# A two-layer float32 decoder trunk: factors 1 and 5 of the seven-product down projection in the mixers' score tiles, block sums in tiles of their own, rotary tables five chunks later

## The chip, the core and the metric

The kernel runs on one core of one Trainium2 chip. A core has a matrix engine (TensorE, PE in the profile), a vector engine (DVE), a scalar engine (ACT) and a general engine (POOL), with one instruction queue each and an on-chip memory that they share; SP is a fifth queue that here only issues loads. Each queue runs its instructions in the order in which they stand in it, and an instruction waits, with all that is behind it in its queue, for the semaphores of the work that it depends on. Matrix products land in PSUM banks, from which DVE and ACT read.

The metric is the device time of one launch in microseconds (us). The kernel before took 2172.97 us as the median of three runs (2170.84 to 2173.14).

## The reference, cut to what matters

Two layers; x is 512 tokens of width 1024, everything in float32. Weights of a layer are 1024 by 2816 for the gated feed-forward blocks.

```python
def swiglu(x, w_gate, w_up, w_down):
    return (jax.nn.silu(x @ w_gate) * (x @ w_up)) @ w_down

for l in range(DEPTH):                                   # DEPTH = 2
    h = h + 0.5 * swiglu(rmsnorm(h, ffn1_norm[l]), ffn1_w_gate[l], ffn1_w_up[l], ffn1_w_down[l])
    z = rmsnorm(h, mix_norm[l]) @ w_in[l]                # columns go to four mixers
    y_a = mla_mixer(...)                                 # latent attention, rotary phases
    y_b = spatial_gating_mixer(...)
    y_c = hgrn2_mixer(...)                               # gated linear recurrence
    y_d = retention_mixer(...)                           # rotary phases, decay
    h = h + jnp.concatenate([y_a, y_b, y_c, y_d], axis=-1) @ w_out[l]
    h = h + 0.5 * swiglu(rmsnorm(h, ffn2_norm[l]), ffn2_w_gate[l], ffn2_w_up[l], ffn2_w_down[l])
    gate = jax.nn.sigmoid(rmsnorm(h, ple_norm[l]) @ ple_w_gate[l])
    h = h + (p[l] @ ple_w_proj[l]) * gate
return rmsnorm(h, final_norm)
```

## The kernel before, in words

**Layout and precision.** The residual stream h lies on chip as eight tiles of 128 features by 512 tokens. Every dense product is made of three float32r products: each operand is split into a rounded high part (a cast, on ACT) and a low rest (a subtraction, on DVE); `parts` (L126) does this, and `mm3` (L171) issues high x high, high x low and low x high (L173, L174, L175).

**Feed-forward block.** `ffn` (L290) walks 22 chunks of 128 hidden features, in parts of 8, 8 and 6 (`PARTS`). `hidden` (L298) makes one chunk: two weight loads of 512 KB by `weights` (L131, SP queue), split into wh and wl, 24 matmuls each for gate and up into the PSUM tiles `gu`, and four evacuation steps (L309 to L312). There are four PSUM banks for them, so the gate product of a chunk can start only when L309 of the chunk two before has read its bank. Parts of 8 chunks go to `down7` (L316), the part of 6 to a plain down projection. There are four feed-forward blocks, so `down7` runs eight times.

**The down projection in seven products.** `down7` multiplies the hidden features with the down weights in 2 by 2 blocks with seven block products instead of eight. The right factors are made of the hidden chunks: hb1 carries those of products 1 and 5, hb2 of 2 and 3, hb3 of 6 and 7, hb4 of 4 (L318 to L337). hb1 is done with the first four chunks; hb2, hb3 and hb4 need the last four. The left factors are weight blocks and sums of them; `seven` (L142) makes them for one pair of output tiles, i and i + 4, and there are four pairs. It loads the two halves of the first block row into a `raw` tile (r1, r2), two of the blocks of the second row into s1 and s3, adds a second block to each of s1 and s3 with an accumulating load on POOL's queue (L157, L158), and loads a last block into a22. `keep` (L146) then splits each factor into a tile `ws` of 128 by 1024, high and low side by side; between these, DVE adds s1 to r1 (L162) and r1 to r2 (L165). Factor 1 is r1, 5 is s1, 2 is r2, 6 is r1 + s1, 3 is r2 + r1 + s1, 7 is s3, 4 is a22. A product is 12 matmuls (L353) into dx, dy or dz, and DVE adds each result to h (L359).

The 28 products stand in an order written by hand (L361): (1,0), (5,0), (1,1), (5,1), (2,0), (6,0), (3,0), (7,0), (2,1), (4,0) and so on, product and pair.

**Tiles.** A pool tag has a fixed number of buffers, and a tile waits until a buffer of its tag is free. Tag `w` has 6 buffers (weights wh and wl, and factors 1, 5, 2, 4); `raw` has 3; `st` has 4 (the mixers' score tiles, and factors 6, 3, 7); `t` has 7 tiles of 128 by 512 (g, gq, squares, and s1, s3, a22); `r` has 3 (row scales, and the token positions while the tables are made); `vx` has 1 and `sc` has 2 (mixers).

**The order of work.** A scheduler orders each queue when the program is built, by priority and by when it expects buffers and results; weights and their splits are marked urgent (L98). So the place of an instruction follows from the buffers too.

**Rotary tables.** `tables` (L389) makes three sine tables and four products of them, on DVE, ACT and one memset on POOL. It runs once, called in the first feed-forward block when chunk 4 has been made (L313), and the mixers use it.

Of the kernel before, what the change touches and what calls it, by code (L numbers as in the profile page):

```python
# [10 lines left out]
F32 = mybir.dt.float32  # L11
F32R = mybir.dt.float32r
# [7 lines left out]
P = 128  # L20
D = 1024
T = 512
# [8 lines left out]
HS = 4  # L31
# [19 lines left out]
WB = 1024  # L51
# [9 lines left out]
def trunk(ctx, tc, xT, pT, pos, wgu, wdn, winT, winN, wout, wpg, wpp, wmla,  # L61
# [8 lines left out]
    tp = ctx.enter_context(tc.tile_pool(name="temps", bufs=1))  # L70
# [5 lines left out]
    def nm(s):  # L76
        uid[0] += 1
        return f"{s}{uid[0]}"
# [2 lines left out]
        return up.tile(list(shape), dt, tag="u", bufs=24, name=nm(name))  # L81

    def t2(shape=(P, T), dt=F32, name="t"):
        return tp.tile(list(shape), dt, tag="t", bufs=7, name=nm(name))

    def stile(name="st"):
        return tp.tile([P, 10, P], F32, tag="st", bufs=4, name=nm(name))
# [32 lines left out]
    def wtile(name):  # L120
        return wp.tile([P, WB], F32R, tag="w", bufs=6, name=nm(name))

    def rtile():
        return wp.tile([P, WB], F32, tag="raw", bufs=3, name=nm("wr"))

# [16 lines left out]
    def seven(a1, a2):  # L142

        w = {}

        def keep(n, p, src):  # L146
            t = wtile("ws") if n % 7 < 4 else tp.tile([P, 10 * P], F32R, tag="st", bufs=4, name=nm("ws"))
            w[p] = t[:, 0:WB].rearrange("p (e c) -> p e c", e=2)
            parts(w[p][:, 0], w[p][:, 1], src)

        with urgent():
            s1, s3, raw, a22 = t2(name="s1"), t2(name="s3"), rtile(), t2(name="a22")
            r1, r2 = raw[:, 0:T], raw[:, T:WB]
            nc.sync.dma_start(out=s1, in_=a2[:, 0:T])
            nc.sync.dma_start(out=s3, in_=a1[:, 0:T])
            nc.sync.dma_start(out=raw, in_=a1)
            nc.gpsimd.dma_start(out=s1, in_=a2[:, T:WB], accum_op=ALU.add)  # L157
            nc.gpsimd.dma_start(out=s3, in_=a2[:, 0:T], accum_op=ALU.add)  # L158
            nc.sync.dma_start(out=a22, in_=a2[:, T:WB])
            keep(0, 1, r1)  # L160
            keep(1, 5, s1)
            dve.tensor_tensor(r1, r1, s1, op=ALU.add)  # L162
            keep(2, 2, r2)
            keep(4, 6, r1)
            dve.tensor_tensor(r2, r2, r1, op=ALU.add)  # L165
            keep(5, 3, r2)
            keep(6, 7, s3)
            keep(3, 4, a22)
        return w

    def mm3(o, a, b, start, stop, go_on=False):  # L171
# [51 lines left out]
    def row_rsqrt(acc, n, last=None, v=None):  # L223

        a = [t2(dt=F32R, name="ac") for _ in range(2)]
        act.copy(a[0], acc)
        dve.tensor_tensor(a[1], acc, a[0].bitcast(F32), op=ALU.subtract)
        q = mps("ms")
        for i in range(2):
            pe.matmul(q, lhsT=onesr, rhs=a[i], start=i == 0, stop=i == 1)  # L230
        return ln_rsqrt(q, n, tp.tile([P, T], F32, tag="r", bufs=3, name=nm("r")), last,
                        v is not None and (v, t2(name="rt")))

    def ln_rsqrt(q, n, r, last=None, vt=None):

        v, t = vt or (t2(name="rv"), t2(name="rt"))
        dve.tensor_scalar(v, q, 1.0 / n, EPS, op0=ALU.mult, op1=ALU.add)
        i = act.preload_act_table_set("natural_log_exp_and_others")
        if last is not None:
            after(i, last)  # L240
        after(act.activation(t, v, AF.Ln), i)
        after(act.activation(r, t, AF.Exp, scale=-0.5), i)
        newton_step(v, r, t)
        return r
# [10 lines left out]
    class Norm:  # L255
# [20 lines left out]
        def scale(self, cols=False):  # L276
            with urgent():
                if not cols:
                    self.r = row_rsqrt(self.acc, D, self.last)
                    return self.r  # L280
                self.vx = tp.tile([P, T], F32, tag="vx", bufs=1, name=nm("vx"))
                self.r = row_rsqrt(self.acc, D, self.last, v=self.vx)
                c = columns(self.r, "rc")
                c2 = sp.tile([P, NB], F32, tag="rc2", bufs=1, name=nm("rc2"))
                dve.tensor_tensor(c2, c, c, op=ALU.mult)
                self.rc = [c, c2]
            return self.r


    def ffn(idx, norm, done, first=None, nextw=None, hook=None):  # L290
        x = norm.x
        r = norm.scale()
        rh = tp.tile([P, T], F32, tag="r", bufs=3, name=nm("rh"))
        act.mul(rh, r, 0.5)
        H = T // 2
        lo_, hi_ = slice(0, H), slice(H, T)
# [1 line left out]
        def hidden(f, g):  # L298
            ps = []
            for m in range(2):  # L300
                if first:
                    ps.append(first.pop(0))
                    continue
                w = nextw.pop(0) if nextw else weights(wgu[idx, f, m])
                o = dense("gu")
                for k in range(KD):
                    mm3(o, wpart(w, k * P), xpart(x[k]), k == 0, k == KD - 1)
                ps.append(o)
            dve.tensor_tensor(g, ps[0], r, op=ALU.mult)  # L309
            act.activation(g, g, AF.Silu)  # L310
            dve.tensor_tensor(g, g, ps[1], op=ALU.mult)  # L311
            dve.tensor_tensor(g, g, rh, op=ALU.mult)  # L312
            if f == 4 and hook is not None:  # L313
                hook()

        def down7(f0):  # L316
# [50 lines left out]
        for n in PARTS:  # L367
# [9 lines left out]
            for m in range(KD):  # L377
                w = weights(wdn[idx, m, :, f0 * P:(f0 + n) * P], n * P)
# [9 lines left out]

    def tables():  # L389
        pin = t2((P, T), I32, name="pin")  # L390
        posf = tp.tile([P, T], F32, tag="r", bufs=3, name="posf")
        nc.scalar.dma_start(out=pin, in_=pos)
        dve.tensor_copy(posf, pin)

# [76 lines left out]
    def mixers(l, norm, done):  # L471
        x = norm.x
        r = norm.scale(True)
# [96 lines left out]
        class Hgrn:  # L570
# [3 lines left out]
            def __init__(self, b, q, kk, ff, wait):  # L574
                self.b, self.q, self.k = b, q, kk
                self.st = stile("hst")[:, 0:8].rearrange("p (e j) t -> p e (j t)", e=2)
                pool.memset(self.st, 0.0)
                self.sc = tp.tile([P, 8, 32], F32, tag="sc", bufs=2, name=nm("sc"))
                dve.tensor_tensor(self.sc, self.near(wait),
                                  cs[:, K_D32:K_D32 + 32].unsqueeze(1).to_broadcast([P, 8, 32]), op=ALU.mult)  # L580
                dve.tensor_tensor(q, q, ff, op=ALU.mult)
                self.d = ff.rearrange("p e t -> p (e t)")
                self.d2 = stile("hd").rearrange("p a t -> p (a t)")
                self.at = 0
# [258 lines left out]
        for b in range(2):  # L843
            pts = []
            for e in range(2):
# [3 lines left out]
                for i in range(NB):  # L849
                    n = (i + 1) * P  # L850
# [42 lines left out]
        for b in range(2):  # L893
            st = [ret_scores(rq_[64 * e:64 * e + 64, b], rk_[64 * e:64 * e + 64, b]) for e in range(2)]
# [2 lines left out]
        yd = group_norm(od, norm.vx, C_RET + 2 * l)  # L897


        rw = t2((P, 256), name="rows")  # L900
        nc.scalar.dma_start(out=rw, in_=rows[l])
        ws = t2((P, HS, P), name="ws")
        after(nc.scalar.dma_start(out=ws, in_=sgw[l]), mla_end)
        bs = sp.tile([P, HS], F32, tag="bs", bufs=1, name=nm("bs"))
        nc.scalar.dma_start(out=bs, in_=sgb[l])
# [41 lines left out]
        for m in range(KD):  # L947
            w = weights(wout[l, m])
# [99 lines left out]
    for _ in range(20):  # L1048
        pe.matmul(o[:, 0:2 * P], lhsT=wide[:, 0:P], rhs=wide, start=True, stop=True)
    raw = [rtile() for _ in range(2)]  # L1050
    hi, lo = ([wtile(f"w{c}0") for _ in range(2)] for c in "hl")
    first = [dense("gu") for _ in range(2)]
    prev = None
    for k in range(KD):
        prev = inturn(nc.sync.dma_start(out=h[k], in_=xT[:, k, :]), prev)
        norm.x[k] = split(h[k], gain(V_FFN1, k))
        for m in range(2):
            if k % 2 == 0:
                c = slice(k * P, (k + 2) * P)
# [4 lines left out]
    with urgent():  # L1064
        for m in range(2):
            w, hi, lo = unit(shape=(P, WB), name="wr"), wtile("wh1"), wtile("wl1")
            for k in range(0, KD, 4):
                c = slice(k * P, (k + 4) * P)
# [133 lines left out]
```

## Time and profile before

| what | value |
|---|---|
| runs | 2172.97 us median, 2170.84 to 2173.14 (3 runs) |
| the profiled execution | 2168.55 us |
| its span on the core | 2166.8 us, 30799 instructions |
| busy, PE / DVE / ACT / POOL | 2105.4 / 1386.0 / 885.5 / 77.3 us |
| mean granted TensorE clock | 0.988 |
| moved by DMA | 224.65 MB |

The page of the profile gives, for one execution on the chip, busy times by engine, the chain of work that ended last, and groups of instructions. "PE gu L173" is a matmul into tile gu at line 173; "dy<-hb,ws" is a product that reads hb and ws. In a list of waits, "PE dy L173 <- ACT ws L127: 26.6, 8, 3.3" says that PE stood still before a matmul of line 173 into dy until ACT had finished a cast into ws, 26.6 us in all, 8 times, 3.3 us at most. In a timeline a row is start, duration, engine, line, operation, and in brackets the idle time before it and what ended it. In a row of windows, PEclk is the granted clock (1.00 is full speed), and "DMA share" the busy share of the core's 16 DMA engines.

### The profile page before, as it was taken

The numbers are of one execution on the slowest core, as the hardware profiler recorded it, in microseconds if no ns is written. First come the engines' busy times: TensorE is split into PE (matmuls) and PEld (weight loads), VectorE is DVE, ScalarE is ACT, GpSimd is POOL, SyncE is SP. The second block draws the span as 40 slices with busy tenths as digits, with TensorE's granted clock in tenths as the row PEclk, the third lists the DMA queues.
The fourth block names the chain that finished last, engine by engine and source line by source line (L and its number), as shares of the span: only waits on it lengthen the run. The fifth ranks groups of instructions, "written<-read, shape, count | busy, mean of one in ns | idle before, by whom it ended". The sixth has DMA issues, their size and how long they took to land.

```text
span 2166.8 us, 30799 instructions
## 1 busy us (share of the span) xinstructions
PE 2105.4 (97%) x12392; PEld 1767.9 (82%) x12392; DVE 1386.0 (64%) x2286; ACT 885.5 (41%) x1379; POOL 77.3 (4%) x109
## 2 busy tenths in 40 slices
PE   8999999999999999999999999999999999999997
PEld 6788888877788798888887988888777888888887
DVE  6775755776675575745766657467766657557476
ACT  5333423625544333423544333245445534233252
POOL 0000100001000000100000001000010001000000
PEclk9999999999999999999999999999999999999999
DMA  4352622322122442523235335232221226235231
GB/s 159 112 139 93 150 98 88 104 73 82 58 78 98 112 132 98 147 96 98 98 107 139 105 111 142 84 102 93 70 90 45 89 97 154 95 117 132 88 124 52
DMA packets 79375, 224.65 MB, mean 104 GB/s; under 512 B 9472, under 2 KB 13056, under 8 KB 79232
## 3 DMA queue, kind: packets, MB, share of 16 engines
q1 hardware_dynamic: 66320, 200.98, 28.2%
q0 software_dynamic: 10240, 18.88, 5.4%
q10 hardware_dynamic: 2672, 2.82, 0.4%
q8 instruction: 97, 1.59, 0.3%
q14 instruction: 46, 0.38, 0.1%
HBM read 218.45 MB, written 2.10 MB: 102 GB/s over the span
## 4 chain that ended last, share of the span: by engine, by line
PE 92%; DVE 4%; ACT 2%; issue 1%; DMA 0%; SPq 0%; DVEq 0%; ACTq 0%
PE gu L173 15%; PE gu L174 15%; PE gu L175 15%; PE z L173 3%; PE z L174 3%; PE z L175 3%; PE dx L173 3%; PE dx L174 3%; PE dx L175 3%; PE dn L173 2%; PE dn L174 2%; PE dn L175 2%; PE dy L175 2%; PE dy L173 1%; PE dy L174 1%; PE y L173 1%
## 5 line engine op out<-in xcount | busy, mean ns | idle before, releaser
L127 ACT CAST wh<-wr 128x1024 fp32r<-128x1024 f32 (+3 forms) x307 | 307.8, 1004 | 730.8 <-issue 318.2
L173 PE MATMUL gu<-x,wh 128*128 128x512 f32 x1408 | 549.3, 391 | 9.4 <-DVE g L309 6.9
L174 PE MATMUL gu<-x,wh 128*128 128x512 f32 x1408 | 549.7, 391 | 0.2
L175 PE MATMUL gu<-x,wl 128*128 128x512 f32 x1408 | 549.5, 390 | 0.0
L128 DVE TENSOR_TENSOR wl<-wr,wh 128x1024 fp32r<-128x1024 f32 (+3 forms) x307 | 356.5, 1163 | 56.8 <-ACT wh L127 52.0
L173 PEld LDWEIGHTS gu<-x,wh 128*128 128x128 f32 x1408 | 265.3, 188 | 65.5 <-issue 4.0
L174 PEld LDWEIGHTS gu<-x,wh 128*128 128x128 f32 x1408 | 265.4, 189 | 56.5 <-DVE x L203 1.7
L175 PEld LDWEIGHTS gu<-x,wl 128*128 128x128 f32 x1408 | 265.1, 188 | 55.5
L311 DVE TENSOR_TENSOR g<-g,gu 128x512 f32<-128x512 f32 x88 | 60.4, 687 | 285.4 <-PE gu L175 279.6
L173 PE MATMUL dx<-hb,ws 128*128 128x256 f32 x512 | 147.1, 288 | 1.2 <-DVE h L359 1.2
L174 PE MATMUL dx<-hb,ws 128*128 128x256 f32 x512 | 146.2, 286 | 0.0
L175 PE MATMUL dx<-hb,ws 128*128 128x256 f32 x512 | 144.6, 285 | 0.0
L309 DVE TENSOR_TENSOR g<-gu,r 128x512 f32<-128x512 f32 x88 | 60.6, 689 | 113.4 <-PE gu L175 113.3
L173 PE MATMUL z<-x,wh 128*128 128x512 f32 x320 | 127.8, 399 | 0.0
L174 PE MATMUL z<-x,wh 128*128 128x512 f32 x320 | 126.6, 396 | 0.0
L175 PE MATMUL z<-x,wl 128*128 128x512 f32 x320 | 126.2, 394 | 0.0
L127 ACT CAST hb<-g 128x256 fp32r<-128x256 f32 (+1 forms) x128 | 58.7, 459 | 138.7 <-DVE g L312 90.1
L127 ACT CAST ws<-wr 128x512 fp32r<-128x512 f32 x128 | 78.8, 619 | 73.6 <-PE gu L174 27.8
L173 PE MATMUL dy<-hb,ws 128*128 128x256 f32 x256 | 77.6, 303 | 26.6 <-ACT ws L127 26.6
L173 PEld LDWEIGHTS dx<-hb,ws 128*128 128x128 f32 x512 | 100.2, 196 | 2.1 <-DVE h L359 1.7
L174 PEld LDWEIGHTS dx<-hb,ws 128*128 128x128 f32 x512 | 100.1, 195 | 0.3
L175 PEld LDWEIGHTS dx<-hb,ws 128*128 128x128 f32 x512 | 99.0, 194 | 0.0
(358 smaller groups left out, 3677.8 us busy)
## 6 DMA issues: line engine op xcount, KB each, us to landing
wr<-in_wgu SPq DMA_DIRECT2D x172, 512.0 KB, 3.2
wr<-in_winT SPq DMA_DIRECT2D x40, 512.0 KB, 3.2
wr<-in_wdn SPq DMA_DIRECT2D x32, 512.0 KB, 3.6
s<-in_wdn SPq DMA_DIRECT2D x64, 256.0 KB, 4.2
s<-in_wdn POOLq DMA_DIRECT2D x64, 256.0 KB, 5.2
wr<-in_wdn SPq DMA_DIRECT2D x32, 384.0 KB, 3.1
a<-in_wdn SPq DMA_DIRECT2D x32, 256.0 KB, 3.7
wr<-in_winN SPq DMA_DIRECT2D x16, 512.0 KB, 3.3
```

The lines of the kernel that those rows point to most:

```text
L127: i = act.copy(hi, src)
L128: dve.tensor_tensor(lo, src, hi.bitcast(F32), op=ALU.subtract)
L173: i = pe.matmul(o, lhsT=a[0], rhs=b[0], start=start, stop=False, skip_group_check=go_on)
L174: pe.matmul(o, lhsT=a[0], rhs=b[1], start=False, stop=False, skip_group_check=go_on)
L175: pe.matmul(o, lhsT=a[1], rhs=b[0], start=False, stop=stop, skip_group_check=go_on)
L309: dve.tensor_tensor(g, ps[0], r, op=ALU.mult)
L311: dve.tensor_tensor(g, g, ps[1], op=ALU.mult)
```

## The change

It moves tiles between buffers and one call in time; no arithmetic is added or left out.

- Factors 1 and 5 of a pair go into `st` buffers, the other five into `w` buffers (before: 6, 3, 7 in `st`; 1, 5, 2, 4 in `w`). The weights of the first chunk go into `st` buffers too.
- s1 and s3 get a tag of their own, `side`, with 4 buffers; the mixers' vx, sc, rows and spatial weights and the token positions use it as well. In return `t` has 6 buffers, `r` has 2, and `vx` and `sc` are gone.
- The tables are called at chunk 9 instead of chunk 4 of the first block.

```diff
     def t2(shape=(P, T), dt=F32, name="t"):
-        return tp.tile(list(shape), dt, tag="t", bufs=7, name=nm(name))
+        return tp.tile(list(shape), dt, tag="t", bufs=6, name=nm(name))
...
+    def spare(name):
+
+        return tp.tile([P, 10 * P], F32R, tag="st", bufs=4, name=nm(name))
+
+    def side(shape=(P, T), name="sd"):
+        return tp.tile(list(shape), F32, tag="side", bufs=4, name=nm(name))
...
-        def keep(n, p, src):
-            t = wtile("ws") if n % 7 < 4 else tp.tile([P, 10 * P], F32R, tag="st", bufs=4, name=nm("ws"))
-            w[p] = t[:, 0:WB].rearrange("p (e c) -> p e c", e=2)
+        def keep(p, src, n=1):
+            w[p] = (wtile("ws") if n else spare("ws"))[:, 0:WB].rearrange("p (e c) -> p e c", e=2)
             parts(w[p][:, 0], w[p][:, 1], src)
 
         with urgent():
-            s1, s3, raw, a22 = t2(name="s1"), t2(name="s3"), rtile(), t2(name="a22")
+            s1, s3, raw, a22 = side(name="s1"), side(name="s3"), rtile(), t2(name="a22")
...
-            keep(0, 1, r1)
-            keep(1, 5, s1)
+            keep(1, r1, 0)
+            keep(5, s1, 0)
             dve.tensor_tensor(r1, r1, s1, op=ALU.add)
-            keep(2, 2, r2)
-            keep(4, 6, r1)
+            keep(2, r2)
+            keep(6, r1)
             dve.tensor_tensor(r2, r2, r1, op=ALU.add)
-            keep(5, 3, r2)
-            keep(6, 7, s3)
-            keep(3, 4, a22)
+            keep(3, r2)
+            keep(7, s3)
+            keep(4, a22)
...
-        return ln_rsqrt(q, n, tp.tile([P, T], F32, tag="r", bufs=3, name=nm("r")), last,
+        return ln_rsqrt(q, n, tp.tile([P, T], F32, tag="r", bufs=2, name=nm("r")), last,
...
-                self.vx = tp.tile([P, T], F32, tag="vx", bufs=1, name=nm("vx"))
+                self.vx = side(name="vx")
...
-        rh = tp.tile([P, T], F32, tag="r", bufs=3, name=nm("rh"))
+        rh = tp.tile([P, T], F32, tag="r", bufs=2, name=nm("rh"))
...
-            if f == 4 and hook is not None:
+            if f == 9 and hook is not None:
                 hook()
...
-        posf = tp.tile([P, T], F32, tag="r", bufs=3, name="posf")
+        posf = side(name="posf")
...
-                self.sc = tp.tile([P, 8, 32], F32, tag="sc", bufs=2, name=nm("sc"))
+                self.sc = side((P, 8, 32), "sc")
...
-        rw = t2((P, 256), name="rows")
+        rw = side((P, 256), "rows")
...
-        ws = t2((P, HS, P), name="ws")
+        ws = side((P, HS, P), "ws")
...
-    hi, lo = ([wtile(f"w{c}0") for _ in range(2)] for c in "hl")
+    hi, lo = ([spare(f"w{c}0") for _ in range(2)] for c in "hl")
```

How this moves instructions is shown at three places. The first is the start of SP's queue; h are the input tiles, wr the first weights, s the blocks s1 and s3 of the first `down7`. Before:

```order
L1055 DMA h_76<-in_xT 128x512
L1060 DMA wr_119<-in_wgu 128x256
L1060 DMA wr_120<-in_wgu 128x256
L138 DMA wr_376<-in_wgu 128x1024
L1055 DMA h_77<-in_xT 128x512
```

And with the change:

```order
L160 DMA s_826<-in_wdn 128x512
L161 DMA s_827<-in_wdn 128x512
L160 DMA s_887<-in_wdn 128x512
L161 DMA s_888<-in_wdn 128x512
L1061 DMA h_76<-in_xT 128x512
L1066 DMA wr_119<-in_wgu 128x256
L1066 DMA wr_120<-in_wgu 128x256
```

Four loads of 256 KB now stand ahead of the first input tile, since their buffers are free from the beginning; on POOL's queue the four accumulating loads that belong to them stand directly behind the memsets at the start.

The second place is ACT's queue at the end of the chunks of the second `down7`: g_1850 and g_1927 are the hidden chunks 14 and 15, hb their right factors, wr_2006 and s_2004 the sources of pair 0's left factors. Before:

```order
L310 ACTIVATE g_1927<-g_1927 128x512
L127 CAST hb_1405<-g_1927 128x512
L127 CAST hb_1409<-gq_1996 128x512
L127 CAST hb_1411<-g_1927 128x256
L127 CAST ws_2017<-s_2004 128x512
L127 CAST ws_2021<-wr_2006 128x512
L127 CAST ws_2024<-wr_2006 128x512
L127 CAST ws_2034<-a_2007 128x512
```

With the change, where ws_2017 (factor 5 of pair 0) stands 15 rows ahead of the last Silu, ahead of this piece:

```order
L134 CAST ws_2021<-wr_2006 128x512
L134 CAST ws_2024<-wr_2006 128x512
L134 CAST hb_1342<-g_1850 128x512
L134 CAST hb_1346<-gq_1919 128x512
L134 CAST hb_1349<-g_1850 128x256
L134 CAST ws_2028<-wr_2006 128x512
L134 CAST ws_2031<-s_2005 128x512
L316 ACTIVATE g_1927<-g_1927 128x512
L134 CAST ws_2255<-wr_2247 128x512
L134 CAST hb_1343<-g_1927 128x512
L134 CAST ws_2258<-s_2245 128x512
L134 CAST ws_2395<-wr_2387 128x512
```

Six of pair 0's seven factors and factors 1 and 5 of pair 1 are now split before the last chunk ends; what stands there after it is the left factors of pairs 2 and 3.

The third place is ACT's queue around the first sine table (tabM). Before it stands among the chunks of the first `down7`:

```order
L392 DMA pin_585<-in_pos 128x512
L310 ACTIVATE g_518<-g_518 128x512
L127 CAST wh_736<-wr_735 128x1024
L127 CAST hb_298<-g_518 128x512
L127 CAST wh_767<-wr_766 128x1024
L406 ACTIVATE tabM<-ang_590 128x512
```

With the change it stands behind that `down7`'s last left factor and the first weights of the next chunks:

```order
L134 CAST ws_1234<-s_1208 128x512
L134 CAST ws_1237<-a_1210 128x512
L134 CAST wh_1351<-wr_1350 128x1024
L412 ACTIVATE tabM<-ang_1492 128x512
L134 CAST wh_1382<-wr_1381 128x1024
L134 CAST wh_1422<-wr_1421 128x1024
```

PE's own queue is the same row for row except at the eight `down7`, where products of pairs 0 and 1 follow each other in another order.

## The prediction

> **What bounds the kernel now.** The page first: the busy row of the engines and the chain that ended last.
>
> ```profile
> PE 2105.4 (97%) x12392; PEld 1767.9 (82%) x12392; DVE 1386.0 (64%) x2286; ACT 885.5 (41%) x1379; POOL 77.3 (4%) x109
> PE 92%; DVE 4%; ACT 2%; issue 1%; DMA 0%; SPq 0%; DVEq 0%; ACTq 0%
> ```
>
> PE bounds it; time can only go where PE stands still or runs slowly. So next the list of waits on PE:
>
> ```profile
> PE dy L173 <- ACT ws L127: 26.6, 8, 3.3
> PE dy L175 <- DVE ws L128: 7.2, 8, 0.9
> PE gu L173 <- DVE g L309: 6.9, 2, 3.6
> ```
>
> The first two are one place, met in each of the eight `down7`: product 5 of pair 0 waits for its left factor, 33.8 us in all. The third is two places: one at the start, one behind the tables. Then the clock, in windows around the eight places (two rows show 0.76, six 0.88):
>
> ```profile
> 108.00:122.00 14.00, 9.80 (x53) 9.24 (x53) 12.40 (x23) 7.96 (x15) 3.48 (x4) 0.76 0.72 180
> 244.00:258.00 14.00, 9.73 (x64) 9.24 (x63) 12.92 (x25) 8.27 (x16) 2.71 (x4) 0.88 0.71 148
> ...
> 1951.00:1965.00 14.00, 9.74 (x65) 9.23 (x64) 12.88 (x25) 8.29 (x16) 2.70 (x4) 0.88 0.71 158
> ```
>
> PE's timeline at the first place shows what that does: before the wait matmuls of 256 columns start 0.12 us apart, after it 0.21.
>
> ```profile
> 109.33 0.28 PE L175 MATMUL dx<-hb,ws 128*128 128x256 f32 x1
> 109.45 0.28 PE L173 MATMUL dx<-hb,ws 128*128 128x256 f32 x1
> ...
> 113.59 0.39 PE L173 MATMUL dy<-hb,ws 128*128 128x256 f32 x1 [3.26 <-ACT ws L127]
> ...
> 116.05 0.41 PE L173 MATMUL dy<-hb,ws 128*128 128x256 f32 x1
> 116.26 0.41 PE L174 MATMUL dy<-hb,ws 128*128 128x256 f32 x1
> ```
>
> So a wait of 3.3 us costs more than itself: a slow stretch follows. The Trainium skill (TensorE: Matmul & The Clock Gate, Part 1: The HAM clock gate) says the same, half speed after about 3.4 us of idle until about 3.4 us of work; this trace agrees, its rows 0.76 and 0.88 being 6.7 us and 3.4 us at half speed in 14.
>
> **Term A, the eight down projections.** First and last of the eight stages, from the first product to the next chunk's first matmul, and two products in steady run:
>
> ```profile
> 108.74 0.28 PE L173 MATMUL dx<-hb,ws 128*128 128x256 f32 x1
> ...
> 157.37 0.40 PE L173 MATMUL gu<-x,wh 128*128 128x512 f32 x1
> ```
> ```profile
> 1951.47 0.28 PE L173 MATMUL dx<-hb,ws 128*128 128x256 f32 x1
> ...
> 1990.82 0.28 PE L173 MATMUL dx<-hb,ws 128*128 128x256 f32 x1
> 1992.26 0.28 PE L173 MATMUL dy<-hb,ws 128*128 128x256 f32 x1
> ...
> 1998.02 0.40 PE L173 MATMUL gu<-x,wh 128*128 128x512 f32 x1
> ```
>
> The first takes 48.6 us, the last 46.6, all eight 376.4. 28 products at 1.44 are 40.3; eight times that is 322.6. So 53.8 us is what can go: 33.8 of waiting, about 15 of slow clock (33.6 us at half speed, in each of which 1 - 0.12/0.21 = 0.44 is lost), the rest small.
>
> Does it go? In the new order factors 1 and 5 of pairs 0 and 1 are split one to two chunks (of 5.4 us: 24 matmuls at 0.227) before the last chunk ends. Their `st` buffers are free, their sources come through `side`, which the chunks' g and gq don't use. So PE has four products, 5.7 us, from buffers that are ready; then the chain of the last hidden chunk is what is late next. Costs of its steps:
>
> ```profile
> L128 DVE TENSOR_TENSOR ws<-wr,ws 128x512 fp32r<-128x512 f32 x128 | 84.6, 685 | 8.5 <-ACT ws L127 7.6
> L127 ACT CAST ws<-wr 128x512 fp32r<-128x512 f32 x128 | 78.8, 619 | 73.6 <-PE gu L174 27.8 <-PE dx L175 24.0 <-DVE wr L165 12.6
> ```
> ```profile
> 118.51 0.68 DVE L128 TENSOR_TENSOR ws<-s,ws 128x512 fp32r<-128x512 f32 x1
> 119.11 0.41 DVE L359 TENSOR_TENSOR h<-h,dy 128x256 f32<-128x256 f32 x1
> 119.44 0.68 DVE L128 TENSOR_TENSOR ws<-s,ws 128x512 fp32r<-128x512 f32 x1
> ```
>
> In a full queue a 512-wide DVE step takes 0.60 from start to start, a 256-wide one 0.33. From the end of the chunk: two steps of g that follow each other (1.4), then hb2 of chunk 15 as the fourth step behind them: ready at 3.5, needed after 57 matmuls, at 6.8. hb3 needs the second half of gq, which stands behind 17 steps after g (11 of 512, 6 of 256; some wait for PE): done at 10.7, cast at 11.3, low part at about 12.3. In the new order PE comes to the cast after 96 matmuls, at 11.5, and to the low part after 104, at 12.4. Residue 0 to 0.5 us a place; I take 0.4, so 3, and for the upper end 1.5 a place, 12. A: -53.8 + 3 = -51.
>
> ACT waits in this order for `st` buffers that PE frees (pair 2's factor 1 at 1.5 us), and hb of chunk 15 stands behind; that is in the 3.5 above. From `w` a pair now takes five tiles instead of four; the last pair takes them as pair 2's products end, and the next chunk's wl finds its buffer when product 6 of pair 3 ends, four products (5.8 us) ahead of its use, covered. On SP the next `down7`'s s loads now stand between the next chunks' weights and hold them until pair 3's sums have been split; by the same adding that is some 10 us before the fourth chunk's weights are used. On POOL the memset of tabM, which waits for DVE, now has one accumulating load behind it that is needed only some 60 us later.
>
> **Term B, the tables.** Where they stand now DVE is full (7.09 of 8.00 us) and L309 comes late to free a bank:
>
> ```profile
> 84.00:92.00 8.00, 7.57 (x34) 5.94 (x32) 7.09 (x13) 3.23 (x5) 0.00 (x0) 1.00 0.60 206
> ```
> ```profile
> 95.16 0.76 PE L173 MATMUL gu<-x,wh 128*128 128x512 f32 x1 [3.59 <-DVE g L309]
> 95.72 0.63 PE L174 MATMUL gu<-x,wh 128*128 128x512 f32 x1
> ...
> 100.42 0.53 PE L173 MATMUL gu<-x,wh 128*128 128x512 f32 x1
> ...
> 102.39 0.39 PE L175 MATMUL gu<-x,wl 128*128 128x512 f32 x1
> 102.62 0.39 PE L173 MATMUL gu<-x,wh 128*128 128x512 f32 x1
> ```
>
> 3.6 us, then 11 matmuls in 4.70 instead of 11 x 0.23 = 2.5: 5.8 in all. Moved, the tables' 15 us of DVE (estimated: some 30 steps at about 0.5) run among the last products and into chunks 8 and 9. Adding the steps in their new order, L309 of chunk 8 comes about 54 us after the first product; PE needs that bank at 40.3 + 4 x 5.4 = 62. I take 1 us of residue: B -5; bounds -5.8 and 0 (the stall back in the new place).
>
> **Term C, the start.** The window of the first 20 us, SP's first issues, the last input's low part, and a stretch in which four loads of s, factor blocks, and four accumulating loads run by themselves (DMA queues of 234 to 250 us):
>
> ```profile
> 0.00:20.00 20.00, 16.33 (x67) 11.54 (x68) 11.78 (x22) 13.76 (x27) 0.84 (x8) 1.00 0.81 253
> ```
> ```profile
> 0.74 0.40 SPq L1055 DMA_DIRECT2D h<-in_xT  x1
> 1.19 0.89 SPq L1060 DMA_DIRECT2D wr<-in_wgu  x2
> ...
> 18.14 0.74 DVE L203 SCALAR_TENSOR_TENSOR x<-h,vec,x 128x512 fp32r<-128x512 f32 x1
> ```
> ```profile
> q0 software_dynamic: 576, 1.05, 45.4%
> q1 hardware_dynamic: 606, 1.09, 18.4%
> ```
>
> PE's matmul on the last input stands right behind the row at 18.14, and the DMA engines are busy 0.81 of that time: the start is bound by loads, and delays pass on. Four loads of s (1.05 MB) go ahead of the first input: 0.184 x 16 us = 2.9. The four accumulating loads on POOL follow as these land and run beside the inputs: 0.454 x 16 = 7.3 if they take the engines' time, 0 if they only fill gaps (20 x 0.19 = 3.8 is idle, half of it before the first byte). No load is taken away, so no gain is possible; C is between +2.5 and +10.2, and up to 1.7 more if the longer wait sets off a half-speed stretch. I take +7, the accumulating loads mostly in the way.
>
> A rule speaks for the dear end: the Trainium skill (DMA: Bandwidth & Descriptors, Queues, rings and completion order) says that each DMA engine takes turns between the queues that have work. By it the accumulating loads would share every engine with the inputs, C would be about +10 and the sum 3 us less; no run here shows it at the start.
>
> The rest I cost at nothing (+-1): `t` with six buffers has lost more tiles than buffers, row scales live at most two at a time, and DVE's and PE's rows in the mixers stand as before.
>
> **The sum.** The profiled execution took 2168.55 us; -51 - 5 + 7 = -49 gives 2119.5. The median of the runs lies 4.4 above that execution, so 2172.97 - 49 = 2124.
>
> **Rivals.**
>
> 1. *The wait only moves.* PE then waits at hb3 (the 11.5 above), say 2 us with 1.5 of slow clock, at each place: 8 x 3.5 = 28 stays. For it: DVE is busy 12.4 to 12.9 of 14 us in the rows above. Against: 8.4 us of its splits and sums there (11 splits, 3 sums at 0.60) now come earlier. Sum -60 + 28 + 7 = -25: 2148. Chance 0.12.
> 2. *The tables stall in their new place.* For it: DVE takes their 15 us on top of a full down projection. B is 0: -44, 2129. Chance 0.12.
> 3. *Slower: the block sums come late.* Pair 2's s1 needs a `side` buffer of pair 0, then a load and an accumulating load:
>
> ```profile
> s<-in_wdn SPq DMA_DIRECT2D x64, 256.0 KB, 4.2
> s<-in_wdn POOLq DMA_DIRECT2D x64, 256.0 KB, 5.2
> ```
>
> Its cast (ws_2258) stands on ACT ahead of pair 1's factor 2 and of hb3. With the buffer freed 19 us before the chunk ends, the sum lands 8 us before that end. If the buffer came free so late that it landed 12 us after the end, PE would stand 5 us at each place and lose 2.6 by the clock: 7.6 a place where it loses 6.7 now, A +7; with -5 and +7: 2182. It decides against the change from (53.8 + 5 - 7)/8 = 6.5 us a place. Against it are some 17 us of slack. Chance 0.03.
> 4. *The change does not do what it says.* The queues show the factors earlier; 0.01 for no difference.
>
> Forecast 0.72, 2124; its own range runs from A -53.8, B -5.8, C +2.5 (2116) to residues of 12 and C +11 (2136). The range 2113 to 2142 adds rival 2 and the runs' spread of 2 us at each side, and leaves out rival 1's middle and rival 3. A measurement of this kernel tells 0.2% (4.3 us) from no change. Faster 0.95, same 0.02, slower 0.03.
>
> **What would show it.** In the profile after: no row "PE dy <- ACT ws" among PE's waits, the windows at the eight places at clock 1.00, each `down7` near 40.5 us; no stall at chunk 6 behind L309, and none at chunks 10 and 11; the first input issued on SP near 2.5 instead of 0.74, and the last one's low part near 25 instead of 18.1. Wrong, if PE waits at hb3 or for `ws` of pairs 1 to 3 by more than 1 us a place, if the clock falls again behind each chunk's end, or if the start loses more than 11 us.

## The result and the profile after

The changed kernel took 2118.98 us (median of four runs, 2116.66 to 2119.19), the kernel before beside it 2173.05 (four runs, 2170.84 to 2175.87): the ratio is 0.9748, 95% interval 0.9731 to 0.9765. The profiled execution has a span of 2117.2 us where before had 2166.8: 49.6 less. The lines of the code stand further down, by seven in `parts` (L127 is L134, L128 is L135) and by six behind `keep` (L173 is L179, L309 is L315, L359 is L365).

The busy row and the chain of the changed kernel:

```profile
PE 2090.1 (99%) x12392; PEld 1755.5 (83%) x12392; DVE 1387.9 (66%) x2286; ACT 883.6 (42%) x1379; POOL 77.0 (4%) x109
PE 93%; DVE 3%; ACT 1%; DMA 1%; issue 1%; SPq 0%; DVEq 0%; ACTq 0%; POOLq 0%
```

PE's waits in the changed kernel:

```profile
PE gu L179 <- ACT wh L134: 3.6, 2, 3.1
PE gu L179 <- DVE g L315: 3.4, 1, 3.4
PE gu L179 <- ACT x L208: 3.0, 1, 3.0
...
PE dx L179 <- ACT hb L134: 0.3, 1, 0.3
```

The two rows of dy, 33.8 us before, are gone, and so is one of the two waits for g. What is left on top lies in the first 45 us, and is new there in part (3.6 for wh). Now the eight down projections, each from its first product to the next chunk's first matmul, as windows (span, busy of PE, PEld, DVE, ACT, POOL, then clock, DMA share, GB/s), with their sum:

```profile
110.73:151.27 40.54, 40.54 (x337) 40.41 (x336) 39.68 (x81) 17.25 (x27) 5.25 (x6) 1.00 0.58 145
...
868.11:909.15 41.04, 40.75 (x337) 40.42 (x336) 32.30 (x62) 16.51 (x26) 5.18 (x6) 1.00 0.59 149
...
1907.67:1948.35 40.68, 40.68 (x337) 40.42 (x336) 32.30 (x62) 16.51 (x26) 1.73 (x2) 1.00 0.35 101
sum 325.06, PE 324.77 PEld 323.37 DVE 265.72 ACT 133.39 POOL 35.01; mean PE 40.60 PEld 40.42 DVE 33.21 ACT 16.67 POOL 4.38
```

Eight stages take 325.1 us instead of 376.4, all at full clock, and 28 products at 1.44 would be 322.6. The start, as a timeline of SP, POOL, DVE and PE:

```profile
0.74 0.40 SPq L160 DMA_DIRECT2D s<-in_wdn  x1
...
2.60 0.43 SPq L1061 DMA_DIRECT2D h<-in_xT  x1
```
```profile
3.96 1.01 POOL L163 DMA_DIRECT2D s<-in_wdn  x1 [2.50 <-DMA s<-in_wdn]
...
6.37 1.28 POOL L164 DMA_DIRECT2D s<-in_wdn  x1
```
```profile
24.63 0.75 DVE L209 SCALAR_TENSOR_TENSOR x<-h,vec,x 128x512 fp32r<-128x512 f32 x1
```
```profile
43.72 0.75 PE L179 MATMUL gu<-x,wh 128*128 128x512 f32 x1 [3.37 <-DVE g L315]
```

And PE's first matmul of chunk 2 in the kernel before, which has the same wait ahead of it:

```profile
35.29 0.50 PE L173 MATMUL gu<-x,wh 128*128 128x512 f32 x1 [3.29 <-DVE g L309]
```

So the first input is issued at 2.60, the last input's low part comes at 24.63 instead of 18.14, and chunk 2 starts 43.72 - 35.29 = 8.4 us later. From there to the first product PE needs 110.73 - 43.72 = 67.0 us where it needed 108.74 - 35.29 = 73.4: the stall behind the tables is gone, 6.4. The balance is -51.4 (stages) - 6.4 (tables) + 8.4 (start) = -49.4 of the 49.6.

### The profile page after: what moved, and what is told of

The parts are those of the page before. It is cut to its first block, busy times and chain, and to the rows that moved or that the text cites. A ratio compares the mean times of both kernels' runs of the same rounds, so it can differ in the third digit from the quotient of the medians.

```text
span 2117.2 us, 30818 instructions
## 1 busy us (share of the span) xinstructions
PE 2090.1 (99%) x12392; PEld 1755.5 (83%) x12392; DVE 1387.9 (66%) x2286; ACT 883.6 (42%) x1379; POOL 77.0 (4%) x109
## 4 chain that ended last, share of the span: by engine, by line
PE 93%; DVE 3%; ACT 1%; DMA 1%; issue 1%; SPq 0%; DVEq 0%; ACTq 0%; POOLq 0%
PE gu L179 15%; PE gu L180 15%; PE gu L181 15%; PE z L179 3%; PE z L180 3%; PE z L181 3%; PE dx L179 3%; PE dx L180 3%; PE dx L181 3%; PE dn L179 2%; PE dn L180 2%; PE dn L181 2%; PE dy L181 1%; PE dy L179 1%; PE dy L180 1%; PE y L179 1%
## 5 line engine op out<-in xcount | busy, mean ns | idle before, releaser
L134 ACT CAST wh<-wr 128x1024 fp32r<-128x1024 f32 (+3 forms) x307 | 307.9, 1004 | 717.4 <-issue 330.7
L179 PE MATMUL gu<-x,wh 128*128 128x512 f32 x1408 | 550.3, 391 | 9.9 <-ACT wh L134 3.6
L135 DVE TENSOR_TENSOR wl<-wr,wh 128x1024 fp32r<-128x1024 f32 (+3 forms) x307 | 356.8, 1163 | 57.8 <-ACT wh L134 53.8
L179 PEld LDWEIGHTS gu<-x,wh 128*128 128x128 f32 x1408 | 265.7, 189 | 67.4 <-ACT wh L134 4.9
L179 PE MATMUL dx<-hb,ws 128*128 128x256 f32 x512 | 144.2, 285 | 0.3 <-ACT hb L134 0.3
L180 PE MATMUL dx<-hb,ws 128*128 128x256 f32 x512 | 144.3, 283 | 0.0
L181 PE MATMUL dx<-hb,ws 128*128 128x256 f32 x512 | 144.2, 283 | 0.0
L134 ACT CAST ws<-wr 128x512 fp32r<-128x512 f32 x128 | 78.5, 619 | 138.3 <-PE dx L181 84.5
L315 DVE TENSOR_TENSOR g<-gu,r 128x512 f32<-128x512 f32 x88 | 60.6, 689 | 103.0 <-PE gu L181 102.9
L179 PE MATMUL z<-x,wh 128*128 128x512 f32 x320 | 127.7, 399 | 0.0
L179 PEld LDWEIGHTS dx<-hb,ws 128*128 128x128 f32 x512 | 97.4, 191 | 2.0 <-ACT hb L134 0.5
L180 PEld LDWEIGHTS dx<-hb,ws 128*128 128x128 f32 x512 | 98.0, 191 | 0.3
L181 PEld LDWEIGHTS dx<-hb,ws 128*128 128x128 f32 x512 | 98.1, 192 | 0.0
L134 ACT CAST hb<-g 128x256 fp32r<-128x256 f32 (+1 forms) x128 | 58.8, 459 | 93.6 <-DVE g L318 45.1
L135 DVE TENSOR_TENSOR ws<-wr,ws 128x512 fp32r<-128x512 f32 x128 | 87.5, 689 | 11.4 <-ACT ws L134 11.2
```

The costliest lines, as they stand in the source:

```text
L134: i = act.copy(hi, src)
L135: dve.tensor_tensor(lo, src, hi.bitcast(F32), op=ALU.subtract)
L179: i = pe.matmul(o, lhsT=a[0], rhs=b[0], start=start, stop=False, skip_group_check=go_on)
L180: pe.matmul(o, lhsT=a[0], rhs=b[1], start=False, stop=False, skip_group_check=go_on)
L181: pe.matmul(o, lhsT=a[1], rhs=b[0], start=False, stop=stop, skip_group_check=go_on)
```

## The experiments

Three edits went into one kernel. Runs 1 to 4 and 8 to 10 take them apart, 5 and 6 the start, and 7 and 11 go after the wait that is left at chunk 2. Every run was timed beside the kernel before on its own chip; the changed kernel's ratio is 0.9748. Runs 1 to 4, 5 to 8 and 9 to 11 each shared a chip, and their medians compare directly.

| run | us, median | ratio to before, 95% interval | eight stages, us |
|---|---|---|---|
| placement alone, on before | 2200.87 | 1.0142 [1.0122, 1.0163] | 411.9 |
| side tiles alone, on before | 2122.31 | 0.9780 [0.9767, 0.9794] | 326.6 (14 matmuls of the first run ahead) |
| tables alone, on before | 2164.66 | 0.9973 [0.9962, 0.9985] | 378.9 |
| change, tables back at chunk 4 | 2119.59 | 0.9766 [0.9753, 0.9780] | 321.5 (part of the first runs ahead) |
| change, s loads later | 2110.55 | 0.9723 [0.9710, 0.9736] | 324.7 |
| change, accumulating loads later | 2114.68 | 0.9742 [0.9729, 0.9755] | 326.5 |
| s loads later, cast behind Exp | 2109.39 | 0.9718 [0.9705, 0.9731] | 324.9 |
| change, first weights in w | 2118.15 | 0.9756 [0.9743, 0.9769] | 324.7 |
| change without the placement | 2123.96 | 0.9778 [0.9765, 0.9792] | 327.3 |
| change with three side buffers | 2133.86 | 0.9823 [0.9809, 0.9838] | 342.4 |
| s loads later, row scale passes | 2105.29 | 0.9694 [0.9681, 0.9707] | 324.5 |

**1. The placement alone.**

```diff
-            t = wtile("ws") if n % 7 < 4 else tp.tile([P, 10 * P], F32R, tag="st", bufs=4, name=nm("ws"))
+            t = wtile("ws") if p not in (1, 5) else tp.tile([P, 10 * P], F32R, tag="st", bufs=4, name=nm("ws"))
```

> The kernel before (2173 us) with one part of the change: factors 1 and 5 of a pair in st buffers, the other five in w; s1 and s3 still in t, tables still at chunk 4. Theory S (the wait for product 5's factor comes from s1's buffer in t, so the side tiles remove it and the placement only supplies cover): factor 5 still stands behind the last chunk's hb on ACT, dy waits about 3 us in each down7, stages stay 46 to 48 us, 2169 to 2177 in all. Theory P (the placement removes it): stages 40.6, all 51 us gone, 2122.

It lost 31 us. PE's waits:

```profile
PE dy L173 <- ACT ws L127: 26.6, 8, 3.3
PE dx L173 <- DVE h L359: 25.0, 14, 4.8
```

The first row is that of before to the tenth, so the placement removes nothing of it, as theory S said. The second row is new, and neither theory had it. PE waits for DVE to add a product to h and free its bank; DVE stands behind a split whose cast ACT hasn't made, and ACT waits for a block sum, 71.5 us in all (5.3 us in the kernel before):

```profile
ACT ws L127 <- DMA s<-in_wdn: 71.5, 16, 7.4
```

This is the mechanism of the third rival, late sums, and with s1 and s3 in t it comes true: 411.9 - 376.4 = 35.5 us over the eight stages, in a profiled execution that took 2207.32, 6.5 above the median.

**2. The side tiles alone** (s1, s3 and the mixers' tiles in `side`, six `t`, two `r`; the tables and the first weights as before, and the factors as before):

```diff
-            w[p] = (wtile("ws") if n else spare("ws"))[:, 0:WB].rearrange("p (e c) -> p e c", e=2)
+            w[p] = (wtile("ws") if p in (1, 5, 2, 4) else spare("ws"))[:, 0:WB].rearrange("p (e c) -> p e c", e=2)
...
-            if f == 9 and hook is not None:
+            if f == 4 and hook is not None:
```

(against the changed kernel, whose first weights go back to w here as well).

> The kernel before with the other part: s1 and s3 (and the mixers' tiles) in side, six t and two r buffers; factors placed as before (1, 5, 2, 4 in w), first weights in w, tables at chunk 4. Theory S: pair 0's two factors are ready when the last chunk ends, the dy row is gone; pair 1's stand behind the last hb, so only two products cover, residue 0 to 3 us a place: stages 40.6 to 43.6, 2122 to 2146. Theory B (both moves are needed): a wait of 3 us moves to pair 1's factors or to hb3 and the clock falls behind it, stages near 46, 2165 or more.

The stages take 326.6 us, 49.8 less than before: nearly all of the 51.4 comes with the side tiles. (In the first stage 14 matmuls, 1.7 us at 0.12, run ahead between 92 and 100 us and aren't in this sum; run 9, where none does, has 327.3.) The wait of dy for ws is met twice only, at 92 and 99 us, where the tables still stand:

```profile
PE dy L179 <- ACT ws L134: 4.1, 2, 3.1
```

**3. The tables alone, on the kernel before.**

```diff
-            if f == 4 and hook is not None:
+            if f == 9 and hook is not None:
```

> The kernel before with the tables called at chunk 9 instead of 4 and nothing else. Theory: the stall of 3.6 us at 91 to 95 us and the 13 slow matmuls behind it go, 6.3 us, and the new place is covered: 2166.7. Rival (the stall goes along): 2173. The first input is issued at 0.74 as before in both.

Gained 5.0 us by the medians, by the interval 3.3 to 8.2; from chunk 2 to the first product 67.0 us instead of 73.4. The window in which DVE was full before has DVE at 4.17 and PE busy throughout:

```profile
84.00:92.00 8.00, 8.00 (x37) 6.60 (x36) 4.17 (x8) 2.75 (x5) 0.00 (x0) 1.00 0.51 157
```

**4. The changed kernel with the tables back at chunk 4** (the same line, the other way).

> The changed kernel (2119 us) with the tables back at chunk 4. In its SP order the s loads then stand behind the inputs again, since the token positions hold a side tile. Theory C (the 8.4 us that the changed kernel loses at the start is the early s loads): +6.3 for the stall, -8.4 for the start, 2117, first chunk-2 matmul near 35.3 us instead of 43.7. Rival (the loss at the start comes from the buffers of the first weights or from something else): 2125.

2119.59: no difference from the changed kernel that can be told (0.9766 against 0.9748). Its trace shows two terms that cancel. The first input is issued at 0.74 and chunk 2 starts at 34.33, 9.4 us earlier, but the stall behind the tables is longer than before:

```profile
34.33 0.79 PE L179 MATMUL gu<-x,wh 128*128 128x512 f32 x1 [3.35 <-DVE g L315]
101.07 0.80 PE L179 MATMUL gu<-x,wh 128*128 128x512 f32 x1 [7.46 <-DVE g L315]
```

From chunk 2 to the end of the first down projection it is 151.44 - 34.33 = 117.1 us against 151.27 - 43.72 = 107.6 in the changed kernel, so the stall costs 9.6 with its slow matmuls, not 6.4. Theory C holds: the early s loads need the side tiles and the move of the tables together (in run 3, with the move alone, chunk 2 starts at 35.61). Read from the order, the token positions hold a side tile when the tables stand at chunk 4, and the s loads then stand behind the weights of chunk 6; that this tile is the reason is argued, not shown.

**5. The s loads behind the inputs.**

```diff
-            nc.sync.dma_start(out=s1, in_=a2[:, 0:T])
-            nc.sync.dma_start(out=s3, in_=a1[:, 0:T])
+            after(nc.sync.dma_start(out=s1, in_=a2[:, 0:T]), gate[0])
+            after(nc.sync.dma_start(out=s3, in_=a1[:, 0:T]), gate[0])
...
+    gate.append(prev)
     for l in range(L):
```

> The changed kernel (2119 us) with one more line: on SP the s loads stand behind the loads of the inputs and of the first two chunks' weights; factors, side tiles and tables as in the change. Theory C (the early s loads cost the start 8.4 to 9.4 us, and nothing needs them before about 60 us): last input's low part at 18 instead of 24.6, chunk 2 at 34 to 35 instead of 43.7, 2109.6 to 2110.6. Rival (something else in the changed kernel delays the start): 2119.

2110.55, as theory C had it; the last input's low part comes at 17.99:

```profile
17.99 0.74 DVE L211 SCALAR_TENSOR_TENSOR x<-h,vec,x 128x512 fp32r<-128x512 f32 x1
```

That is 8.4 us by the medians of two chips, and 7.6 against run 8, which differs from the changed kernel in nothing that counts and shared this chip. In the traces the first product starts at 104.26 instead of 110.73, 6.5 earlier; chunk 2 starts at 36.22, later than the expected 34 to 35, and this profiled execution took 2112.70, 2.2 above the median.

**6. Only the accumulating loads later.**

```diff
+            for s in (s1, s3):
+                after(act.copy(s[:, 0:1], s[:, 0:1]), gate[0])
             nc.gpsimd.dma_start(out=s1, in_=a2[:, T:WB], accum_op=ALU.add)
...
+    gate.append(split_end)
     for l in range(L):
```

> The changed kernel with the plain s loads early as they are, but each accumulating load held until ACT has split the second chunk's weights, by a copy of one column in place (about 24 us). Theory M (the accumulating loads take the engines' time from the inputs, 14.2% of 16 engines in 40 us = 5.7 us; the plain loads cost 2.9): chunk 2 at about 38, 2113.5. Rival G (the accumulating loads fill gaps, the plain loads ahead of the inputs cost it all): chunk 2 at 43.7, 2119.

2114.68, close to theory M. The accumulating loads now start at 21.04 instead of 3.96, the plain s loads stay first, and chunk 2 starts at 37.67, the first product at 104.61: 6.1 us earlier than in the changed kernel and 0.4 later than with all s loads moved. So at the first product it is nearly all the accumulating loads. At the last input's low part (20.43 here, 24.63 in the changed kernel, 17.99 in run 5) they hold 4.2 of 6.6, the plain loads 2.4. By the medians of this chip it is 3.5 of 7.6 (2118.15 in run 8, 2114.68 here, 2110.55 in run 5); the stages of this kernel are 1.7 longer (326.5 against 324.7); if that is the price of the columns copied on ACT, which isn't shown, it is 5.2. The views of the DMA issues of the first 40 us (count, KB each, median us from issue to landing) show what they do to the inputs. The changed kernel:

```profile
h<-in_xT SPq DMA_DIRECT2D x8, 256.0 KB, 7.9
s<-in_wdn POOLq DMA_DIRECT2D x4, 256.0 KB, 9.7
```

This kernel, with the same four plain s loads ahead:

```profile
h<-in_xT SPq DMA_DIRECT2D x8, 256.0 KB, 5.4
s<-in_wdn POOLq DMA_DIRECT2D x4, 256.0 KB, 9.2
```

The inputs take 2.5 us longer to land when the accumulating loads run beside them.

**7. The remaining stall at chunk 2.** In the changed kernel ACT's cast of chunk 2's gate weights stands ahead of the norm's cast and waits for a w buffer, and the row scale for L315 waits with it:

```profile
34.11 1.05 ACT L134 CAST wh<-wr 128x1024 fp32r<-128x1024 f32 x1 [4.09 <-PE gu L180]
35.06 0.62 ACT L232 CAST ac<-acc 128x512 fp32r<-128x512 f32 x1
```

```diff
+        exps.append(after(act.activation(r, t, AF.Exp, scale=-0.5), i))
...
+            i = parts(hi[:, :cols], lo[:, :cols], raw[:, :cols])
+            if behind is not None:
+                after(i, behind)
...
+weights(wgu[idx, f, m], behind=exps[0] if idx == 0 and f == 2 and m == 0 else None)
```

> The kernel of the run before last (s loads behind the inputs) with one more edge: ACT's split of chunk 2's gate weights stands behind the norm's Exp instead of ahead of the norm's cast, where it waits 4.1 us for a w buffer. Theory (that wait is what makes L315 late): the row scale is ready some 4 us earlier, the stall of 3.4 us at chunk 2 and the 13 slow matmuls behind it go, 6.1 us: 2104. Rival (the scale's own chain, or chunk 2's weights, are late by as much): the stall stays, 2110.

Against its theory the stall stayed (3.11 us). By the medians the run is 1.2 us better than run 5 with intervals that overlap, so no gain can be told. In its trace the slow matmuls behind the stall are gone, and from chunk 2 to the first product it takes 99.72 - 34.32 = 65.4 us where run 5 took 104.26 - 36.22 = 68.0; but the first of these executions lies 1.5 below the median of its runs, the second 2.2 above. DVE's timeline shows what took the place of the wait:

```profile
29.48 1.22 DVE L135 TENSOR_TENSOR wl<-wr,wh 128x1024 fp32r<-128x1024 f32 x1
30.62 0.68 DVE L232 SCALAR_TENSOR_TENSOR r<-rt,r 128x512 f32<-128x512 f32 x1
31.22 2.35 DVE L135 TENSOR_TENSOR wl<-wr,wh 128x1024 fp32r<-128x1024 f32 x2
33.49 1.28 DVE L322 TENSOR_TENSOR g<-gu,r 128x512 f32<-128x512 f32 x2
```

Three low parts of weights, made late by the later casts, stand ahead of the step that frees the bank (L322 here): one ahead of the row scale's last step (L232), two behind it.

**8. The first weights back in w.**

```diff
-    hi, lo = ([spare(f"w{c}0") for _ in range(2)] for c in "hl")
+    hi, lo = ([wtile(f"w{c}0") for _ in range(2)] for c in "hl")
```

> The changed kernel with the first chunk's weights back in w buffers instead of st. The order of all queues is the same; only buffers differ. Theory: chunk 1's up weights wait for a w buffer of the first gate product, as in the kernel before (0.7 us on ACT, beside other work): 2119 to 2120. Rival (the six w buffers were part of the 8.4 us at the start, or are needed for it): off by 2 us or more.

2118.15: no difference. This part of the change is worth nothing by itself.

**9. The change without the placement** (factors as before, the first line of run 2's diff alone).

> The changed kernel with the factors placed as before (1, 5, 2, 4 in w, 6, 3, 7 in st); side tiles, tables at chunk 9 and first weights as in the change. Theory S (the side tiles alone remove the wait, the placement is worth what the stages of the run with side tiles alone lack, 326.6 against 325.1 us): 2120 to 2121. Rival (the placement carries part of the gain once the tables are out of the way): a wait of over 1 us at each of eight places, 2127 or more.

2123.96, a ratio of 0.9778 against 0.9748, with intervals that just touch: the placement is worth some 5 us by the medians, more than theory S gave and less than its rival. The spans of the two profiled executions differ by 2.6 (2119.8 and 2117.2), and the stages hold 2.2 of that (327.3 against 325.1: two of them 41.5 to 41.6). Where the rest lies is open.

**10. Three side buffers instead of four.**

```diff
-        return tp.tile(list(shape), F32, tag="side", bufs=4, name=nm(name))
+        return tp.tile(list(shape), F32, tag="side", bufs=3, name=nm(name))
```

> The changed kernel with three side buffers instead of four, so pair 1's s3 has to wait for a buffer of pair 0. Theory (only s1 is needed before the last chunk ends; s3 feeds product 7, nine or more products later; one early load less at the start gives some of the 8 us back): 2116 to 2119. Rival L (late sums, as in the run with the placement alone: PE waits at 'dx <- DVE h' while ACT stands behind a sum that has not landed): 2 us a place or more, 2135.

Rival L was right and the theory wrong: 2133.86, with the same chain as in run 1. PE's row, and one of ACT's waits in the last stage:

```profile
PE dx L179 <- DVE h L365: 14.0, 8, 2.6
```
```profile
1934.03 1.14 ACT L134 CAST ws<-s 128x512 fp32r<-128x512 f32 x2 [1.93 <-DMA s<-in_wdn]
```

With one buffer less a sum lands late in each of the eight places, and the stages grow by 17.4 us.

**11. The row scale passes on both engines.** As run 7, but the gate's cast stands between the norm's cast and its Ln, its low part behind the norm's first DVE step, and the up weights behind Exp and the first L315:

```diff
+        if behind:
+            after(i, behind[0])
+            after(j, behind[1])
...
+                late = (acs[0], rvs[0]) if m == 0 else (exps[0], gs[0])
+                w = nextw.pop(0) if nextw else weights(wgu[idx, f, m], behind=late if idx == 0 and f == 2 else None)
```

> The late s loads again, and now both engines let the row scale pass: on ACT chunk 2's gate split stands between the norm's cast and its Ln, the up split behind Exp; on DVE the gate's low part stands behind the norm's first step, the up's behind the first L315. Theory (in the run with the Exp edge three low parts of 1.1 us stood ahead of L315, so the stall stayed): chunk 2 starts near 31 instead of 34.3, its wait under 1 us, 2106. Rival (the scale's own chain from the last square is as long as the two chunks that cover it): 2109, the stall stays.

2105.29, better than both kernels and than every other run; 0.9694 against 0.9723 for run 5, which lacks only these edges. No wait for g is left on PE; chunk 2 starts 0.35 us after the matmul ahead of it:

```profile
33.37 0.39 PE L186 MATMUL gu<-x,wl 128*128 128x512 f32 x1
33.72 0.47 PE L184 MATMUL gu<-x,wh 128*128 128x512 f32 x1
```

It comes at 33.7 and not at 31, because in this execution the start ran slower than in run 7 (last section): by 17 us PE had started 25 matmuls of the first two chunks, there 37. That PE came later isn't why the wait is gone. From DVE's first step on the norm's sum (the first row is run 7, the second this run) to chunk 2's first matmul it is 33.72 - 28.58 = 5.1 us here and 34.32 - 26.03 = 8.3 in run 7, of which PE works 5.2 and waits 3.1:

```profile
26.03 0.69 DVE L250 TENSOR_SCALAR rv<-ms 128x512 f32<-128x512 f32 x1 [2.13 <-PE ms L241]
28.58 0.69 DVE L251 TENSOR_SCALAR rv<-ms 128x512 f32<-128x512 f32 x1 [4.14 <-PE ms L244]
```

## Why the prediction was right, step by step

**Term A** was -51 and is -51.4. The residue of 0.4 us a place is 0.3 ((325.1 - 322.6)/8). The step that it rests on held to 0.2 us: hb3's cast was put at 11.3 us after the last chunk's end and PE's arrival at 11.5. In the last stage (ACT, then PE):

```profile
1918.59 0.62 ACT L134 CAST hb<-gq 128x512 fp32r<-128x512 f32 x1 [0.34 <-DVE gq L339]
1919.11 0.61 ACT L134 CAST ws<-s 128x512 fp32r<-128x512 f32 x1
```
```profile
1919.06 0.28 PE L181 MATMUL dx<-hb,ws 128*128 128x256 f32 x1
1919.26 0.51 PE L179 MATMUL dx<-hb,ws 128*128 128x256 f32 x2
```

The cast ends 11.5 us after 1907.67 and PE's next matmul starts at 11.6, 0.20 behind the one before it where 0.12 is its pace: there is no slack. In the fourth stage the first rival (the wait moves to hb3) did come, in small. ACT waited there for a block sum, hb3's cast started 11.3 us after the first product instead of 10.8, and PE waited for it:

```profile
875.62 0.62 ACT L134 CAST ws<-s 128x512 fp32r<-128x512 f32 x1 [1.29 <-DMA s<-in_wdn]
879.39 0.62 ACT L134 CAST hb<-gq 128x512 fp32r<-128x512 f32 x1 [0.70 <-DVE gq L339]
```
```profile
880.06 0.50 PE L179 MATMUL dx<-hb,ws 128*128 128x256 f32 x2 [0.29 <-ACT hb L134]
```

That stage took 41.04 us where most took 40.56. The prediction gave two reasons for the early factors in one breath, free st buffers and sources through `side`. Runs 1, 2 and 9 separate them: the side tiles bring 49.1 of it (376.4 - 327.3, run 9), the placement by itself does harm, and with the side tiles it adds 2 in the stages and 5 in all. The slow clock went with the wait, as it said: 1.00 in all eight windows.

**Term B** was -5 and is -6.4, above the bound of -5.8. The slow stretch was under-counted: 13 matmuls ran slow, not 11, with the first and last of the stretch partly so, 2.7 us instead of 2.2. The residue of 1 us in the new place isn't there: from the first down projection to the second, 238.34 - 151.27 = 87.1 us, is what before took without the tables (244.43 - 157.37). What the prediction didn't see is that B and C hang together: the tables' move brings the early s loads (run 4). Inside this change it is worth nothing net; alone on the kernel before, 5.

**Term C** was +7 and is +8.4. The accumulating loads were taken as about 4 of the 7 and the plain loads as 2.9; by runs 5, 6 and 8 the accumulating ones cost 5.2 (medians) to 6.1 (trace), and the plain ones 0.4 to 2.4. C came out between its two bounds, nearer to the upper one. The rule by which engines take turns between queues (the Trainium skill, DMA: Bandwidth & Descriptors, Queues, rings and completion order) gave +10; this trace agrees with it better than with gap filling, by the inputs' 7.9 against 5.4 us to landing. The extra of up to 1.7 for a slow stretch came too: 6.5 of the 8.4 is there at the last input, the other 1.9 comes behind it. PE had then started 33 matmuls of the first two chunks, in the kernel before 39; at 0.23 these six are 1.4 us of work left over, and the rest is open.

**The sum** came out at 2119.5 for the profiled execution; that took 2118.98. The number on record, 2124, is 5 us high by one step: the 4.4 us by which the median of before lay above its profiled execution were carried over, and the changed kernel's profiled execution is itself at its median. So the medians differ by 54.1 us and the two profiled executions by 49.6, and the traces account for the latter alone. That the sum fits to half a us is in part luck: B was 1.4 too small and C 1.4 too small, with opposite signs.

**The rivals.** The tables' stall did not come along. Late sums, the slower rival, came only in small: ACT waited for a block sum in three of the eight stages, 1.29, 0.47 and 0.92 us, and in the fourth PE then waited for hb3 (Term A). None of these is pair 2's s1, for which the prediction counted "some 17 us of slack"; a later sum had none, and run 10 shows how much hangs on the fourth side buffer. With three, 2.2 us a place are lost, and without side tiles (run 1) 4.4.

## What to carry to other kernels

When a factor is late, ask first where its source waits for a buffer: a tag of its own for the sources (run 2) gave what a better place for the results alone (run 1) turned into a loss. Freed buffers also let loads move, so look at the head of every load queue after such a change; here one more ordering edge gave another 7.6 us (run 5 against run 8). And when an engine's queue is in order, freeing one engine of a head-of-line wait may only hand it to the next (run 7), so move the step on each engine that it passes through (run 11).

## What the runs showed of the chip

A wait of some 2.5 us sometimes sets off half pace and sometimes not. In the kernel before PE waited 2.48 us for the second input and its matmuls went on 0.23 us apart soon after; in run 11 it waited 2.42 and they stood 0.43 apart until 15.8:

```profile
8.50:11.00 2.50, 1.28 (x3) 1.00 (x4) 1.30 (x3) 2.06 (x5) 0.00 (x0) 0.61 1.07 361
11.00:14.00 3.00, 3.00 (x8) 2.32 (x8) 3.00 (x7) 3.00 (x8) 0.00 (x0) 0.50 0.91 276
```

The Trainium skill (TensorE: Matmul & The Clock Gate, Part 1: The HAM clock gate) says that the window in which activity is watched runs freely, so that the slow stretch of one kernel varies with its phase; these runs fit that but, being of different kernels, don't show it. At chunk 2 matmuls came 0.30 and then 0.23 apart behind 3.11 us in run 7, and 0.55 and then 0.42 apart behind 3.37 in the changed kernel (the row at 43.72 above).

```profile
34.32 0.47 PE L183 MATMUL gu<-x,wh 128*128 128x512 f32 x1 [3.11 <-DVE g L322]
34.62 0.39 PE L184 MATMUL gu<-x,wh 128*128 128x512 f32 x1
```

This is no border in length. In the down projections, where PE is full ahead of the wait, one of 2.60 us in run 10 set off half pace (0.21 where 0.12 is full; the granted clock between 1806.4 and 1810 is 0.55), and one of 2.72 in run 1 did not. So the "about 3.4 us of idle" in the prediction is no safe lower limit:

```profile
1806.49 0.40 PE L179 MATMUL dx<-hb,ws 128*128 128x256 f32 x1 [2.60 <-DVE h L365]
1807.12 0.41 PE L179 MATMUL dx<-hb,ws 128*128 128x256 f32 x1
1807.33 0.41 PE L180 MATMUL dx<-hb,ws 128*128 128x256 f32 x1
```
```profile
2006.26 0.39 PE L173 MATMUL dx<-hb,ws 128*128 128x256 f32 x1 [2.72 <-DVE h L359]
2006.60 0.28 PE L175 MATMUL dx<-hb,ws 128*128 128x256 f32 x1
2006.71 0.28 PE L173 MATMUL dx<-hb,ws 128*128 128x256 f32 x1
```

The granted clock can miss a slow stretch. In the changed kernel's start the matmuls stand 0.43 apart between 8.5 and 11 and, but for waits, again from 14.4 to 23, and the row says 1.00, as do those of 14 to 23:

```profile
8.50:11.00 2.50, 2.48 (x6) 1.84 (x6) 1.13 (x3) 0.79 (x2) 0.00 (x0) 1.00 1.07 283
```

Six matmuls in 2.5 us is the pace to read there, not the clock's column; why the record lacks it isn't known.
